# Fixed weight slots, in-place raw operands and earlier bank sums in the second MLP product of a hybrid decoder trunk

## The chip, the cores and the metric

The kernel runs on one core of one Trainium2 chip. The metric is device time in microseconds (us) of that core, from the first instruction to the last. Five engines work beside each other: PE multiplies matrices, DVE (vector), ACT (scalar) and POOL work on tiles, and SP does nothing here but issue DMAs. Each engine takes its instructions in the order in which the program lists them; an instruction that waits on another engine or on a DMA holds up all that stand behind it on its own engine.

## The reference

One layer of a decoder trunk: token mixing (pooling, gated DeltaNet and convolution heads between an input and an output projection), then an MLP, then a final normalisation. The change touches the last two:

```python
hf = _rmsnorm(x, g_norm2) * (1 + scale2) + shift2
a = jax.nn.relu(hf @ w_ff1)                 # (2048, 1024) @ (1024, 4096)
x = x + gate2 * ((a * a) @ w_ff2)           # (2048, 4096) @ (4096, 1024)
y = _rmsnorm(x, g_final)                    # x * rsqrt(mean(x*x)) * g_final
```

Everything is fp32. A second input of 8 single rows (the samples) goes through the same weights.

## The kernel before, in words

The two MLP products are done in the Winograd form of Strassen's method: a 2x2 block product takes 7 products (P1, P6, P5, P7, P2, P3, P4) of sums of blocks in place of 8. Each fp32 operand is split in two halves, a rounded high part (an ACT copy) and the rest as low part (a DVE subtraction), and each product is 3 matmuls (high x high, high x low, low x high).

The second product (`a*a` times `w_ff2`) runs in 8 passes (`nb`) over the hidden dimension. A pass takes two row groups of weights (`q` = 0 and 1) and goes over 8 tiles of the output (`gi`, `j`). So there are 64 blocks (function `block`) of 7 products x 2 q x 3 = 42 matmuls of 128x128 by 128x512. The 7 products of a block share four PSUM banks `ps_x`, `ps_y`, `ps_v`, `ps_z`, in the order x, y, v, z, x, v, z; when a bank is done, DVE adds it to a running sum in SBUF (`acc`, `accu`), and only then may the next product use that bank.

What a block reads:

- The weights of the pass, 2 x 7 tiles `wo` of 128x2x512 (B11, B21, B22 and sums T1 to T4). `w2_load` fetches the raw rows, `w2_samples` uses them for the samples (small matmuls into `ps_s`) and scales them by the gate on POOL (L1686), and `w2_ops` makes the sums (POOL, in place) and splits them (ACT cast L1401, DVE subtraction L1398). Each `wo` takes the next slot of a ring of 20 (`RING2`, through `entry`): with 14 tiles a pass, a tile of the next pass reuses the slot of one that the current pass may still be reading.
- The activations, tiles `ai` for each (tile, q), double buffered, two DMAs each (products 0 to 3, products 4 to 6). Where `early` holds (q = 0 nearly always) they come from DRAM already split. For the other half, `a_load` fetches the raw sums into a buffer `af` of its own (double buffered), and ACT and DVE split them into `ai` (L1759, L1398).

In the last pass the first two products' sum `accu` is added to `c22` on DVE and to `c12` and `c21` on POOL. Then the tiles that are finished go in groups through `final`: squares with row sums on ACT (L1798), the inverse root on DVE (a chain of some 13 small instructions), a multiplication by `gf` (the gains `g_final`) on POOL for one half, scaling on ACT (L1816) and DVE (L1818), and an output DMA. `gf`, and `gs`, `accs`, `xr` of the samples, live in the same memory slots as some of the weights (pool `r2`, tag "o", 9 slots before).

A scheduler sets the order of every engine's list: it runs the program through its own model of time and takes, of what is ready there, what has the highest priority (`tc.high_priority`); a tile whose slot is not yet free in that model is not ready.

Of the kernel before, what the change touches and what calls it, by code (L numbers as in the profile page):

```python
# [9 lines left out]
F32 = mybir.dt.float32  # L10
F32R = mybir.dt.float32r
# [6 lines left out]
P = 128  # L18
D = 1024
# [25 lines left out]
XB = 11  # L45
AO = 4
WE = 4
TB = 10
R2 = 9
XS = 1000  # L50
ORDER = ["gp01kq23"] * 4
RSQRT_MAGIC = 1597463007.0
# [9 lines left out]
def hybrid_trunk(  # L62
# [1311 lines left out]
    with ExitStack() as ph2:  # L1374
# [66 lines left out]
        a32 = f1.tile([P, 2, 2, 32], F32, name="a32")  # L1441
        Q.memset(a32, 0.0)
        chunks = f1.tile([P, 256], F32, name="chunks")
        xsT = f1.tile([P, KT, 32], F32, name="xsT")
        Q.memset(xsT, 0.0)


# [99 lines left out]
        def entry(slots):  # L1547
            pool, tag = slots[ring[0] % len(slots)]
            ring[0] += 1
            return pool.tile([P, 2, 512], F32R, tag=tag, name="wo")  # L1550

        RING1 = [(wp, "whi"), (wp, "wlo"), (we, "e"), (we, "e"), (wp, "whi"), (wp, "wlo")] + [(we, "e")] * (WE - 2)

# [105 lines left out]
        KB = 2  # L1659
        NB = NP // KB  # L1660
        halves = (slice(0, 512), slice(512, 1024))
        RING2 = [(wp, "whi")] + [(ao, "a")] * AO + [(xpool, "x"), (wp, "wlo"), (wp, "whi"), (wp, "wlo")]

        def w2_load(p, pool=None):
            raws = []
# [19 lines left out]
                for raw in raws:  # L1685
                    Q.tensor_tensor(out=raw, in0=raw, in1=g2, op=ALU.mult)  # L1686

        def w2_ops(raws):

            with tc.high_priority(offset=HP):  # L1690
                return right_ops(*(raw[:, s] for raw in raws for s in halves), lambda o: entry(RING2))

        with tc.high_priority(offset=800):
            xs_ops = [x_ops_first(j) for j in range(4)]
# [6 lines left out]
        for gi in range(2):  # L1701
            for p in range(NP):
                w_now = w
                if gi == 0 or p < NP - 1:
                    raws = w1_load((p + 1) % NP)
                    if srow:
                        sample_rows(*srow)
                        srow = None
                    if gi or p == NP - 1:
                        srow = sample_unit((p + 1) % NP, raws)  # L1710
                    w = w1_ops(raws)
                if p == 0 and gi:
                    with tc.high_priority(offset=XS):
                        xs_ops = x_second()
                    c = unit(w_now, xs_ops)
                elif p == 0:
                    c = unit_by_k(w_now, lambda j: xs_ops[j])
                else:
                    if gi and p == NP - 1:
                        g2 = xpool.tile([P, D], F32, tag="x", name="g2")  # L1720
                        for k in range(KT):
                            nc.sync.dma_start(out=g2[:, k * P:(k + 1) * P], in_=g2_scr[k, 8:9, :].to_broadcast([P, P]))
                        ring[0] = 0
                        first2 = [w2_load(0), w2_load(1, xpool)]
                        for q in range(KB):
                            w2_samples(q, first2[q])
                        w2 = [w2_ops(first2[0])]
                    c = unit(w_now, xs_ops)
                a_ops(gi, p, c)
                if gi and p == NP - 1:  # L1730
                    sample_rows(*srow)
                if gi == 0 and p in (2, 6, 10):
                    later = (x_later(0), x_later(1), x_sums())[p // 4]
                for _ in later:
                    break
                if gi == 0 and p == 14:
                    xt = load_rows(x1_scr[T:T + NS, :], NS)
                    A.activation(out=xt[:NS], in_=xt[:NS], func=AF.Copy, scale=rs2[:NS, 16:17])
                    full = sample_act(xt, 3, lambda: psa.tile([P, KT, NS], F32, tag="b", name="ps_hs"))
                    V.tensor_copy(out=xsT[:, :, 0:NS], in_=full)  # L1740

        ff1_pools.close()
        ai = ph2.enter_context(tc.tile_pool(name="ai", bufs=2))
        r2 = ph2.enter_context(tc.tile_pool(name="r2", bufs=R2))
        sm = ph2.enter_context(tc.tile_pool(name="sm3", bufs=2))
        ac = ph2.enter_context(tc.tile_pool(name="ac", bufs=1))
        RING2 += [(r2, "o")] * R2 + [(xpool, "x")] * 2

        def a_load(gi, j, p):

            es = [ai.tile([P, n_, 2, P], F32R, tag=f"i{p % 2}{h}", name=f"ai{h}", bufs=2) for h, n_ in enumerate((4, 3))]
            if early(gi, p):
                for e, o in zip(es, (slice(0, 4), slice(4, 7))):
                    nc.sync.dma_start(out=e.bitcast(F32).rearrange("p o a t -> p o (a t)"), in_=a_scr[gi][p][:, j, o])
            else:
                raw = ai.tile([P, 7, P], F32, tag="f", name="af", bufs=2)
                nc.sync.dma_start(out=raw, in_=a_scr[gi][p][:, j])
                for e, o in zip(es, (slice(0, 4), slice(4, 7))):
                    A.copy(out=e[:, :, 0, :], in_=raw[:, o])  # L1759
                    sub(V, e[:, :, 1, :], raw[:, o], e[:, :, 0, :])  # L1760
            return es

        acc = {}
# [10 lines left out]
        def block(nb, gi, j, w, a):  # L1774

            b = {n: bank("ps_" + n) for n in "xyvz"}
            rows, u = acc[gi, j]
            c11, c12, c21, c22 = (r[:, s] for r in rows for s in halves)
            into = {0: u, 1: u, 2: c22, 3: c22, 4: c11, 5: c12, 6: c21}
            for n, ((l, r), name, first, last) in enumerate(PRODUCTS):  # L1780
                ps = b[name]
                for q in range(KB):
                    for i, (x, y) in enumerate(PAIRS):
                        nc.tensor.matmul(out=ps, lhsT=a[q][n // 4][:, n % 4, x, :], rhs=w[q][r][:, y, :],  # L1784
                                         start=first and q == 0 and i == 0, stop=last and q == KB - 1 and i == 2,
                                         skip_group_check=True)
                if n == 0 and nb == 0:
                    A.copy(out=u, in_=ps)
                else:
                    add(V, into[n], ps, into[n])  # L1790
                if n == 1 and nb == NB - 1:
                    add(V, c22, c22, u)
                    add(Q, c12, c12, u)
                    add(Q, c21, c21, u)

        def square_sum(x, out):
            junk = ai.tile([P, 512], F32, tag="junk", name="junk", bufs=1).bitcast(BF16)[:, 0:x.shape[-1]]
# [22 lines left out]
                    nc.sync.dma_start(out=dst[:, s], in_=x[:m, s])  # L1820

        def samples_out():
            gs, accs, xr = (r2.tile([P, D], F32, tag="o", name=n) for n in ("gs", "accs", "xr"))
            nc.sync.dma_start(out=gs[0:NS].rearrange("j (k p) -> j k p", k=KT),
                              in_=g2_scr[:, 0:NS, :].rearrange("k j p -> j k p"))
            for j in range(4):
                nc.sync.dma_start(out=accs[0:NS, 256 * j:256 * j + 256], in_=chunks[32 * j:32 * j + NS])
            load_rows(x1_scr[T:T + NS, :], NS, xr)
            Q.tensor_tensor(out=accs[:NS], in0=accs[:NS], in1=gs[:NS], op=ALU.mult)
            add(V, accs[:NS], accs[:NS], xr[:NS])  # L1830
            final([(accs, NS, y_sample.rearrange("b t d -> (b t) d"))])

        tiles = [(gi, j) for gi in range(2) for j in range(4)]
        w = [w2[0], w2_ops(first2[1])]
        done = []
        steps = [(nb, gi, j) for nb in range(NB) for gi, j in tiles]
        a = [a_load(0, 0, q) for q in range(KB)]
# [1 line left out]
        for i, (nb, gi, j) in enumerate(steps):  # L1839
            a_now, w_now = a, w  # L1840
            if i + 1 < len(steps):
                nb2, gi2, j2 = steps[i + 1]
                a = [a_load(gi2, j2, KB * nb2 + q) for q in range(KB)]
                if nb2 == 0:
                    acc_load(gi2, j2)
            if nb + 1 < NB:
                at = i % len(tiles)
                if at == 0:
                    w_next = []
                if at in (0, 3):  # L1850
                    raws = w2_load(KB * (nb + 1) + at // 3)
                elif at in (2, 5):
                    w2_samples(KB * (nb + 1) + at // 3, raws)
                    w_next.append(w2_ops(raws))
                elif at == len(tiles) - 1:
                    w = w_next
            block(nb, gi, j, w_now, a_now)
            if nb == NB - 1:
                if i == len(steps) - len(tiles):
                    gf = r2.tile([P, D], F32, tag="o", name="gf")  # L1860
                    nc.sync.dma_start(out=gf, in_=g_final.unsqueeze(0).to_broadcast([P, D]))
                if i == len(steps) - len(tiles) + 1:
                    samples_out()
                done += [(acc[gi, j][0][th], P, y_prompt[0, t * P:(t + 1) * P, :])
                         for th, t in enumerate((8 * gi + j, 8 * gi + 4 + j))]
                if j % 2 or gi and j == 2:
                    final(done)
                    done = []
# [27 lines left out]
```

## Time and profile before

| | us |
|---|---|
| three timed runs, median | 2512.17 (2507.35 to 2512.51) |
| profiled execution | 2506.09 |
| its span | 2504.4 |
| first matmul of the second product starts at | 1795.71 |
| last group of 6 matmuls of the second product | 2489.03 to 2491.79 |
| last work of DVE and ACT ends at | about 2500.0 |

Busy shares over the span are PE 95%, DVE 76%, ACT 44%, POOL 28%. The second product takes the last 28% of the span. Times below are from the start of the span. Up to the second product nothing but line and buffer numbers differs between the two kernels' lists, so it is the stretch from 1795 on that has to be read.

### The profile page before, as it was taken

The numbers are of one execution on the slowest core, as the hardware profiler recorded it, in microseconds if no ns is written. First come the engines' busy times: TensorE is split into PE (matmuls) and PEld (weight loads), VectorE is DVE, ScalarE is ACT, GpSimd is POOL, SyncE is SP. The second block draws the span as 40 slices with busy tenths as digits, with TensorE's granted clock in tenths as the row PEclk, the third lists the DMA queues.
The fourth block names the chain that finished last, engine by engine and source line by source line (L and its number), as shares of the span: only waits on it lengthen the run. The fifth ranks groups of instructions, "written<-read, shape, count | busy, mean of one in ns | idle before, by whom it ended". The sixth has DMA issues, their size and how long they took to land. (4 is left out here: it accounts for less than half of the span.)

```text
span 2504.4 us, 36348 instructions
## 1 busy us (share of the span) xinstructions
PE 2369.7 (95%) x12797; PEld 1887.6 (75%) x12797; DVE 1902.9 (76%) x3378; ACT 1092.1 (44%) x2411; POOL 697.9 (28%) x469
## 2 busy tenths in 40 slices
PE   7988999999999999989999999999899999999996
PEld 4566788788999788667877767777677777778775
DVE  3986987887887576677788786766777777777788
ACT  3266247237336443456565665555432112211224
POOL 2101101021111234543236422223513222322254
PEclk9999999999999999999999999999999999999998
DMA  9986534544543567844779785656655455545455
GB/s 326 352 278 226 171 122 167 175 144 160 210 137 131 147 198 228 269 156 147 249 229 324 252 266 156 206 160 197 213 222 168 156 165 158 157 151 159 157 172 178
DMA packets 406150, 490.72 MB, mean 196 GB/s; under 512 B 39082, under 2 KB 306027, under 8 KB 405944
## 3 DMA queue, kind: packets, MB, share of 16 engines
q1 hardware_dynamic: 331120, 386.55, 47.5%
q10 hardware_dynamic: 73088, 96.48, 11.8%
q0 software_dynamic: 1760, 5.38, 0.7%
q8 instruction: 101, 1.65, 0.3%
q14 instruction: 81, 0.66, 0.1%
HBM read 335.63 MB, written 153.07 MB: 195 GB/s over the span
## 5 line engine op out<-in xcount | busy, mean ns | idle before, releaser
L179 PE MATMUL ps_ip<-hhi,whi 128*128 128x512 f32 (+1 forms) x1112 | 411.7, 371 | 11.5 <-ACT whi L150 9.0
L179 PE MATMUL ps_ip<-hhi,wlo 128*128 128x512 f32 (+1 forms) x1112 | 409.8, 369 | 4.9 <-DVE wlo L131 4.9
L179 PE MATMUL ps_ip<-hlo,whi 128*128 128x512 f32 (+1 forms) x1112 | 409.4, 369 | 4.4 <-DVE hlo L131 3.4
L179 PEld LDWEIGHTS ps_ip<-hhi,whi 128*128 128x128 f32 x1112 | 211.6, 190 | 53.4 <-ACT whi L150 11.1
L179 PEld LDWEIGHTS ps_ip<-hhi,wlo 128*128 128x128 f32 x1112 | 211.7, 190 | 45.5 <-DVE wlo L131 10.2
L179 PEld LDWEIGHTS ps_ip<-hlo,whi 128*128 128x128 f32 x1112 | 211.7, 190 | 38.7 <-DVE hlo L131 5.2
L1784 PE MATMUL ps_v<-wo,ai 128*128 128x512 f32 x768 | 203.4, 396 | 19.0 <-DVE acc L1395 10.1
L1401 ACT CAST wo<-raw 128x512 fp32r<-128x512 f32 x208 | 125.6, 618 | 197.4 <-POOL raw L1398 62.6
L1759 ACT CAST ai<-af 128x384 fp32r<-128x384 f32 (+1 forms) x128 | 72.2, 568 | 316.5 <-PE ps_z L1784 268.6
L1784 PE MATMUL ps_x<-wo,ai 128*128 128x512 f32 x768 | 201.1, 401 | 5.8 <-DVE accu L1395 2.6
L1398 DVE TENSOR_TENSOR wo<-raw,wo 128x512 fp32r<-128x512 f32 x208 | 190.7, 930 | 16.3 <-ACT wo L1401 15.8
L1784 PE MATMUL ps_z<-wo,ai 128*128 128x512 f32 x768 | 200.9, 395 | 0.6 <-DVE acc L1395 0.4
L1686 POOL TENSOR_TENSOR raw<-raw,g 128x1024 f32<-128x1024 f32 x32 | 79.5, 2504 | 413.4 <-PE ps_s L1678 195.7
L1570 PE MATMUL ps_v<-xo,wo 128*128 128x512 f32 x744 | 186.5, 398 | 6.0 <-DVE t L1395 4.0
L551 DVE SCALAR_TENSOR_TENSOR dc<-glu,dww,dc 128x512 f32<-128x512 f32 x240 | 190.1, 820 | 1.7
L1398 DVE TENSOR_TENSOR wo<-s,wo 128x512 fp32r<-128x512 f32 x128 | 122.4, 961 | 88.8 <-ACT wo L1401 87.6
L1784 PEld LDWEIGHTS ps_v<-wo,ai 128*128 128x128 f32 x768 | 144.7, 190 | 55.1 <-DVE acc L1395 13.1
L1570 PE MATMUL ps_x<-xo,wo 128*128 128x512 f32 x744 | 185.2, 396 | 0.7 <-ACT s L1611 0.7
L1570 PE MATMUL ps_z<-xo,wo 128*128 128x512 f32 x744 | 183.2, 394 | 2.5 <-DVE t L1395 2.5
L1784 PEld LDWEIGHTS ps_x<-wo,ai 128*128 128x128 f32 x768 | 145.7, 192 | 46.8 <-DVE accu L1395 4.4
L1784 PEld LDWEIGHTS ps_z<-wo,ai 128*128 128x128 f32 x768 | 145.5, 190 | 34.7 <-DVE acc L1395 2.4
L1570 PEld LDWEIGHTS ps_v<-xo,wo 128*128 128x128 f32 x744 | 138.5, 189 | 41.6 <-DVE t L1395 6.0
(503 smaller groups left out, 4709.6 us busy)
## 6 DMA issues: line engine op xcount, KB each, us to landing
a_scr<-ae SPq DMA_DIRECT2D x112, 512.0 KB
raw<-in_w_ff SPq DMA_DIRECT2D x94, 512.0 KB
whi<-w_scr ACTq DMA_DIRECT2D x66, 512.0 KB
wlo<-w_scr ACTq DMA_DIRECT2D x66, 512.0 KB
ai<-a_scr SPq DMA_DIRECT2D x64, 512.0 KB
af<-a_scr SPq DMA_DIRECT2D x64, 448.0 KB
mraw<-in_w_ada SPq DMA_DIRECT2D x48, 512.0 KB
ai<-a_scr SPq DMA_DIRECT2D x64, 384.0 KB
```

What stands on the lines that cost most here:

```text
L179: nc.tensor.matmul(out=ps, lhsT=a[:, k, :], rhs=b, start=(i == 0), stop=(i == 3 * KT - 1))
L551: nc.vector.scalar_tensor_tensor(out=d, in0=gt[:, j:j + GT], scalar=dww[:, t, j:j + 1], in1=d, op0=ALU.mult, op1=ALU.add)
L1398: eng.tensor_tensor(out=out, in0=in0, in1=in1, op=ALU.subtract)
L1401: A.copy(out=entry[:, 0, :], in_=full)
L1570: nc.tensor.matmul(out=ps, lhsT=w[:, a, c], rhs=x[:, b, :], start=start and i == 0, stop=stop and i == 2, skip_group_check=True)
L1686: Q.tensor_tensor(out=raw, in0=raw, in1=g2, op=ALU.mult)
L1759: A.copy(out=e[:, :, 0, :], in_=raw[:, o])
L1784: nc.tensor.matmul(out=ps, lhsT=a[q][n // 4][:, n % 4, x, :], rhs=w[q][r][:, y, :], start=first and q == 0 and i == 0, stop=last and q == ...
```

## The change

It does six things, all in the second product:

1. The ring goes. A pass has fixed slots by its parity: `DOUBLED[0]` for even passes, `DOUBLED[1]` for odd ones, 9 slots each, for the 7 tiles of q = 0 and for B11 and T2 of q = 1. The other five tiles of q = 1 have one slot each (tags s0, s1, ...) for all passes. "o" has 7 slots instead of 9.
2. The raw rows of the next pass are loaded at blocks 1 and 3 of a pass instead of 0 and 3 and used at 2 and 5 as before; in the first pass they are loaded at 1 and 4 and used at 3 and 6.
3. `a_load` has no `af`: the raw sums go by two DMAs straight into the low half of `ai`, ACT casts from there to the high half, and DVE subtracts in place.
4. In the last pass the bank adds on DVE get a priority of 400.
5. There, the add of `accu` to `c22` comes after product 4 instead of after product 1.
6. The tile `xsT` moves to another pool; `gf`, `gs`, `accs`, `xr` stay in tag "o", of which an odd pass, as the last one is, uses all 7.

```diff
-R2 = 9
+R2 = 7
+LP = 400
-        RING2 = [(wp, "whi")] + [(ao, "a")] * AO + [(xpool, "x"), (wp, "wlo"), (wp, "whi"), (wp, "wlo")]
+        DOUBLED = [[(wp, "whi")] + [(ao, "a")] * AO + [(xpool, "x"), (wp, "wlo"), (wp, "whi"), (wp, "wlo")]]
...
-        def w2_ops(raws):
+        def w2_ops(n, raws):
+            slots = DOUBLED[n // KB % 2]
+            b11, b12, b21, b22 = (raw[:, s] for raw in raws for s in halves)
             with tc.high_priority(offset=HP):
-                return right_ops(*(raw[:, s] for raw in raws for s in halves), lambda o: entry(RING2))
+                if n % KB == 0:
+                    ring[0] = 0
+                    return right_ops(b11, b12, b21, b22, lambda o: entry(slots))
...
+                t = ai.tile([P, 512], F32, tag="junk", name="t2", bufs=1)
+                put(B11, b11, slots[7])
+                sub(Q, b11, b12, b11)
+                sub(Q, b12, b22, b12)
+                sub(Q, t, b22, b11)
+                put(T2, t, slots[8])
+                sub(Q, t, b21, t)
+                for o, full in ((T1, b11), (T3, b12), (B21, b21), (B22, b22), (T4, t)):
+                    put(o, full, (r2, f"s{o}"))
+                return out
...
-        r2 = ph2.enter_context(tc.tile_pool(name="r2", bufs=R2))
+        r2 = ph2.enter_context(tc.tile_pool(name="r2", bufs=1))
-        RING2 += [(r2, "o")] * R2 + [(xpool, "x")] * 2
+        DOUBLED.append([(r2, "o")] * 5 + [(xpool, "x")] * 2 + [(r2, "o")] * 2)
...
-                raw = ai.tile([P, 7, P], F32, tag="f", name="af", bufs=2)
-                nc.sync.dma_start(out=raw, in_=a_scr[gi][p][:, j])
-                for e, o in zip(es, (slice(0, 4), slice(4, 7))):
-                    A.copy(out=e[:, :, 0, :], in_=raw[:, o])
-                    sub(V, e[:, :, 1, :], raw[:, o], e[:, :, 0, :])
+                    nc.sync.dma_start(out=e32[:, :, 1, :], in_=a_scr[gi][p][:, j, o])
+                    A.copy(out=e[:, :, 0, :], in_=e32[:, :, 1, :])
+                    sub(V, e[:, :, 1, :], e32[:, :, 1, :], e[:, :, 0, :])
...
-                    add(V, into[n], ps, into[n])
-                if n == 1 and nb == NB - 1:
-                    add(V, c22, c22, u)
+                    with tc.high_priority(offset=LP if nb == NB - 1 else 0):
+                        add(V, into[n], ps, into[n])
+                if nb == NB - 1 and n == 1:
                     add(Q, c12, c12, u)
                     add(Q, c21, c21, u)
+                if nb == NB - 1 and n == 4:
+                    add(V, c22, c22, u)
...
-            gs, accs, xr = (r2.tile([P, D], F32, tag="o", name=n) for n in ("gs", "accs", "xr"))
+            gs, accs, xr = (r2.tile([P, D], F32, tag="o", name=n, bufs=R2) for n in ("gs", "accs", "xr"))
...
-                if at in (0, 3):
-                    raws = w2_load(KB * (nb + 1) + at // 3)
-                elif at in (2, 5):
+                loads, uses = ((1, 4), (3, 6)) if nb == 0 else ((1, 3), (2, 5))
+                if at in loads:
+                    raws = w2_load(KB * (nb + 1) + loads.index(at))
+                elif at in uses:
...
-                    gf = r2.tile([P, D], F32, tag="o", name="gf")
+                    gf = r2.tile([P, D], F32, tag="o", name="gf", bufs=R2)
```

SP's list in the last pass of the kernel before (`a_scr_14` and `a_scr_15` are the activations of the last pass, `out` the results) has the loads of `gf`, `gs`, `accs` and `xr` among the loads of the first tiles, and the first results between later loads:

```order
L1754 DMA ai_22108<-a_scr_14_11322 128x1024
L1861 DMA gf<-in_g_final 128x1024
L1824 DMA gs<-g_scr 8x8x128
L1827 DMA accs<-chunks 8x256 x3
L1754 DMA ai_22112<-a_scr_15_11323 128x1024
L1827 DMA accs<-chunks 8x256
L193 DMA xr<-x_scr 8x1024
L1754 DMA ai_22261<-a_scr_14_11322 128x1024
...
L1754 DMA ai_22445<-a_scr_14_11338 128x1024
L1820 DMA out<-acc_17762 128x512 x2
L1820 DMA out<-acc_17764 128x512 x2
```

In the changed kernel SP has them behind the last load of activations, after everything else of the pass:

```order
L1779 DMA ai_22525<-a_scr_15_11339 128x4x128
L1777 DMA ai_22522<-a_scr_14_11338 128x768
L1779 DMA ai_22526<-a_scr_15_11339 128x3x128
L1777 DMA ai_22641<-a_scr_14_11338 128x1024
L1779 DMA ai_22645<-a_scr_15_11339 128x4x128
L1777 DMA ai_22642<-a_scr_14_11338 128x768
L1779 DMA ai_22646<-a_scr_15_11339 128x3x128
L1885 DMA gf<-in_g_final 128x1024
L1847 DMA gs<-g_scr 8x8x128
```

What moved: `gf` from ahead of the second tile's activations to behind the last tile's. In the last pass the seven "o" slots hold weights of that pass, and each of the four tiles gets one only when a product of the last block has read it.

ACT's list in the last pass of the kernel before has squares (`junk,fv`) and scalings (`nr_y`) between the casts of the activations:

```order
L1759 CAST ai_22449<-af 128x4x128
L1816 ACTIVATE acc_17762<-acc_17762,nr_y 128x512
L1816 ACTIVATE acc_17764<-acc_17764,nr_y 128x512
L1816 ACTIVATE acc_17779<-acc_17779,nr_y 128x512
L1816 ACTIVATE acc_17781<-acc_17781,nr_y 128x512
L1798 ACTIVATE junk,fv<-acc_17924 128x512 x2
L1759 CAST ai_22450<-af 128x3x128
L1798 ACTIVATE junk,fv<-acc_17926 128x512 x2
```

In the changed kernel the last cast comes first, and then all 34 squares and all 17 scalings in one row (its first lines):

```order
L1780 CAST ai_22525<-ai_22525 128x4x128
L1780 CAST ai_22526<-ai_22526 128x3x128
L1780 CAST ai_22645<-ai_22645 128x4x128
L1780 CAST ai_22646<-ai_22646 128x3x128
L1821 ACTIVATE junk,fv<-accs 8x512 x2
L1821 ACTIVATE junk,fv<-acc_17763 128x512 x2
L1821 ACTIVATE junk,fv<-acc_17765 128x512 x2
L1821 ACTIVATE junk,fv<-acc_17780 128x512 x2
L1821 ACTIVATE junk,fv<-acc_17782 128x512
```

What moved: every square and scaling of the final normalisation, from between the blocks of the last pass to behind its last load.

PE's list at the start of the second product, before (`ai_17754` and `ai_17771` are q = 1 of the first two tiles, `ps_s` the samples):

```order
L1784 MATMUL ps_x<-wo,ai_17754 128x512
L1784 MATMUL ps_x<-wo,ai_17771 128x512 x3
L1678 MATMUL ps_s_17929<-raw_17784,a_11341 32x256
L1678 MATMUL ps_s_17929<-raw_17786,a_11341 32x256
...
L1784 MATMUL ps_y<-wo,ai_17754 128x512
L1784 MATMUL ps_y<-wo,ai_17771 128x512
L1784 MATMUL ps_y<-wo,ai_17754 128x512 x2
```

and in the changed kernel (there the two are `ai_17755` and `ai_17772`):

```order
L1805 MATMUL ps_x<-wo,ai_17755 128x512
L1805 MATMUL ps_y<-wo,ai_17755 128x512 x2
L1805 MATMUL ps_x<-wo,ai_17772 128x512 x2
L1805 MATMUL ps_y<-wo,ai_17772 128x512 x2
L1805 MATMUL ps_x<-wo,ai_17772 128x512
L1805 MATMUL ps_y<-wo,ai_17772 128x512
L1679 MATMUL ps_s_18004<-raw_17855,a_11341 32x256
L1679 MATMUL ps_s_18004<-raw_17857,a_11341 32x256
...
L1805 MATMUL ps_v<-wo,ai_17755 128x512
L1805 MATMUL ps_z<-wo,ai_17755 128x512
```

What moved: the six matmuls of `ps_y` for q = 1 (they read the weight tile T2) now stand ahead of the samples' matmuls.

## Rows read from the trace of the kernel before

**Rows 1.** Windows: stretch, its length, busy us (count) by engine, granted clock, DMA share.
```profile
1795.00:1825.00 30.00, 19.48 (x69) 12.71 (x68) 21.05 (x30) 11.99 (x22) 15.85 (x9) 0.77 0.98 348
2066.00:2150.00 84.00, 81.21 (x370) 63.79 (x369) 62.31 (x89) 19.10 (x34) 24.43 (x15) 1.00 0.52 162
2396.00:2492.00 96.00, 80.75 (x324) 62.17 (x322) 90.16 (x152) 37.76 (x91) 53.19 (x37) 0.95 0.49 162
```

**Rows 2.** Waits of PE, 1795 to 2505: total us, times, longest.
```profile
PE ps_v L1784 <- DVE acc L1395: 10.1, 3, 5.8
PE ps_v L1784 <- DVE wo L1398: 8.8, 4, 2.8
PE ps_y L1784 <- ACT wo L1401: 4.4, 4, 2.5
PE ps_s L1678 <- DMA raw<-in_w_ff: 3.2, 1, 3.2
PE ps_x L1784 <- DVE accu L1395: 2.6, 3, 2.0
PE ps_y L1784 <- DVE wo L1398: 2.3, 2, 1.7
```

**Rows 3.** Timeline of PE and ACT, start of the second product: start, us, work.
```profile
1811.22 1.09 PE L1678 MATMUL ps_s<-raw,a 128*32 128x256 f32 x14 [3.21 <-DMA raw<-in_w_ff]
1814.12 2.18 ACT L1401 CAST wo<-raw 128x512 fp32r<-128x512 f32 x4 [8.64 <-DMA af<-a_scr]
1814.79 1.22 PE L1784 MATMUL ps_y<-wo,ai 128*128 128x512 f32 x2 [2.48 <-ACT wo L1401]
```

**Rows 4.** Timeline of DVE and PE at a change of passes.
```profile
1979.55 5.13 DVE L1398 TENSOR_TENSOR wo<-raw,wo 128x512 fp32r<-128x512 f32 x3
1984.73 0.73 PE L1784 MATMUL ps_v<-wo,ai 128*128 128x512 f32 x2 [2.76 <-DVE wo L1398]
...
1985.53 2.89 PE L1784 MATMUL ps_x<-wo,ai 128*128 128x512 f32 x12
1988.26 0.62 PE L1784 MATMUL ps_z<-wo,ai 128*128 128x512 f32 x2
```

**Rows 5.** Groups of DVE: a middle pass (2066 to 2150), then the last (2400 to 2505).
```profile
L1398 DVE TENSOR_TENSOR wo<-raw,wo 128x512 fp32r<-128x512 f32 x16 | 17.3, 1106 | 2.4 <-ACT wo L1401 2.3
...
L1395 DVE TENSOR_TENSOR acc<-acc,accu 128x512 f32<-128x512 f32 x8 | 12.3, 1553 | 0.1
L1395 DVE TENSOR_TENSOR acc<-ps_v,acc 128x512 f32<-128x512 f32 x16 | 10.8, 683 | 1.6 <-PE ps_v L1784 1.5
```

**Rows 6.** Chain that ended last: issue of an activation load, us to its landing.
```profile
2305.02 3.59 DMA ai<-a_scr
2417.24 3.79 DMA ai<-a_scr
```

**Rows 7.** Waits of SP's queue, 1795 to 2400.
```profile
SPq L1754 <- PE ps_z L1784: 260.3, 87, 6.7
```

**Rows 8.** Timeline of ACT and groups of POOL, last pass: squares, scalings, `gf` multiplications.
```profile
2426.15 0.63 ACT L1798 ACTIVATE junk<-acc 128x512 bf16<-128x512 f32 x1
2426.90 0.63 ACT L1798 ACTIVATE junk<-acc 128x512 bf16<-128x512 f32 x1
2440.85 2.56 ACT L1816 ACTIVATE acc<-acc,nr_y 128x512 f32<-128x512 f32 x4 [4.74 <-DVE nr_y L123]
...
L1809 POOL TENSOR_TENSOR acc<-acc,gf 128x512 f32<-128x512 f32 x16 | 21.3, 1334 | 25.4 <-ACT junk L1798 25.2 <-DVE nr_a L121 0.2
```

**Rows 9.** Timeline of the end.
```profile
2489.03 2.76 PE L1784 MATMUL ps_z<-wo,ai 128*128 128x512 f32 x6
2493.47 7.73 SPq L1820 DMA_DIRECT2D out<-acc  x8
2495.27 0.16 DVE L1395 TENSOR_TENSOR sq<-fv 128x2 f32<-128x2 f32 x1 [1.17 <-ACT junk L1798]
2498.66 1.33 ACT L1816 ACTIVATE acc<-acc,nr_y 128x512 f32<-128x512 f32 x2 [3.42 <-DVE nr_y L123]
```

More of the change, by code (lines that the diff above doesn't have):

```diff
@@ L1443, in hybrid_trunk @@
         chunks = f1.tile([P, 256], F32, name="chunks")
-        xsT = f1.tile([P, KT, 32], F32, name="xsT")
+        xsT = sm.tile([P, KT, 32], F32, name="xsT", bufs=1)
         Q.memset(xsT, 0.0)
@@ L1549, in entry @@
             ring[0] += 1
-            return pool.tile([P, 2, 512], F32R, tag=tag, name="wo")
+            return pool.tile([P, 2, 512], F32R, tag=tag, name="wo", **({"bufs": R2} if tag == "o" else {}))
         RING1 = [(wp, "whi"), (wp, "wlo"), (we, "e"), (we, "e"), (wp, "whi"), (wp, "wlo")] + [(we, "e")] * (WE - 2)
@@ L1686, in w2_samples, with put @@
                     Q.tensor_tensor(out=raw, in0=raw, in1=g2, op=ALU.mult)
-        def w2_ops(raws):
+        def w2_ops(n, raws):
+            slots = DOUBLED[n // KB % 2]
+            b11, b12, b21, b22 = (raw[:, s] for raw in raws for s in halves)
             with tc.high_priority(offset=HP):
-                return right_ops(*(raw[:, s] for raw in raws for s in halves), lambda o: entry(RING2))
+                if n % KB == 0:
+                    ring[0] = 0
+                    return right_ops(b11, b12, b21, b22, lambda o: entry(slots))
+                out = {}
+                def put(o, full, pool_tag):
+                    pool, tag = pool_tag
+                    out[o] = pool.tile([P, 2, 512], F32R, tag=tag, name="wo", **({"bufs": R2} if tag == "o" else {}))
+                    split(out[o], full)
+                t = ai.tile([P, 512], F32, tag="junk", name="t2", bufs=1)
[8 more added lines that the diff above has]
+                return out
         with tc.high_priority(offset=800):
@@ L1726, in hybrid_trunk @@
                             w2_samples(q, first2[q])
-                        w2 = [w2_ops(first2[0])]
+                        w2 = [w2_ops(0, first2[0])]
                     c = unit(w_now, xs_ops)
@@ L1743, in hybrid_trunk @@
         ai = ph2.enter_context(tc.tile_pool(name="ai", bufs=2))
-        r2 = ph2.enter_context(tc.tile_pool(name="r2", bufs=R2))
+        r2 = ph2.enter_context(tc.tile_pool(name="r2", bufs=1))
         sm = ph2.enter_context(tc.tile_pool(name="sm3", bufs=2))
         ac = ph2.enter_context(tc.tile_pool(name="ac", bufs=1))
-        RING2 += [(r2, "o")] * R2 + [(xpool, "x")] * 2
+        DOUBLED.append([(r2, "o")] * 5 + [(xpool, "x")] * 2 + [(r2, "o")] * 2)
         def a_load(gi, j, p):
             es = [ai.tile([P, n_, 2, P], F32R, tag=f"i{p % 2}{h}", name=f"ai{h}", bufs=2) for h, n_ in enumerate((4, 3))]
-            if early(gi, p):
-                for e, o in zip(es, (slice(0, 4), slice(4, 7))):
-                    nc.sync.dma_start(out=e.bitcast(F32).rearrange("p o a t -> p o (a t)"), in_=a_scr[gi][p][:, j, o])
-            else:
-                raw = ai.tile([P, 7, P], F32, tag="f", name="af", bufs=2)
-                nc.sync.dma_start(out=raw, in_=a_scr[gi][p][:, j])
-                for e, o in zip(es, (slice(0, 4), slice(4, 7))):
-                    A.copy(out=e[:, :, 0, :], in_=raw[:, o])
-                    sub(V, e[:, :, 1, :], raw[:, o], e[:, :, 0, :])
+            for e, o in zip(es, (slice(0, 4), slice(4, 7))):
+                e32 = e.bitcast(F32)
+                if early(gi, p):
+                    nc.sync.dma_start(out=e32.rearrange("p o a t -> p o (a t)"), in_=a_scr[gi][p][:, j, o])
+                else:
+                    nc.sync.dma_start(out=e32[:, :, 1, :], in_=a_scr[gi][p][:, j, o])
+                    A.copy(out=e[:, :, 0, :], in_=e32[:, :, 1, :])
+                    sub(V, e[:, :, 1, :], e32[:, :, 1, :], e[:, :, 0, :])
             return es
@@ L1833, in hybrid_trunk @@
         tiles = [(gi, j) for gi in range(2) for j in range(4)]
-        w = [w2[0], w2_ops(first2[1])]
+        w = [w2[0], w2_ops(1, first2[1])]
         done = []
@@ L1849, in hybrid_trunk @@
                     w_next = []
-                if at in (0, 3):
-                    raws = w2_load(KB * (nb + 1) + at // 3)
-                elif at in (2, 5):
-                    w2_samples(KB * (nb + 1) + at // 3, raws)
-                    w_next.append(w2_ops(raws))
+                loads, uses = ((1, 4), (3, 6)) if nb == 0 else ((1, 3), (2, 5))
+                if at in loads:
+                    raws = w2_load(KB * (nb + 1) + loads.index(at))
+                elif at in uses:
+                    w2_samples(KB * (nb + 1) + uses.index(at), raws)
+                    w_next.append(w2_ops(KB * (nb + 1) + uses.index(at), raws))
                 elif at == len(tiles) - 1:
```

## The prediction

> **What bounds the kernel now.** I read the windows first, to see which engine is full in which stretch. In a middle pass of the second product PE is busy 81 of 84 us at the full granted clock, DVE 62; from 2396 to 2492, the last pass, DVE is busy 90 of 96 us while PE's clock falls to 0.95 of full [rows 1]. So PE sets the time in the middle, and at two kinds of places something else does. The waits of PE say which: bank sums on DVE (`acc`, 10.1 us in three waits), weight splits on DVE and ACT (8.8, 4.4, 2.3), the `accu` add (2.6), one load of raw weights (3.2) [rows 2]. The timelines then place them: the start, the change of passes, the last pass, the end.
>
> A matmul takes 0.2275 us at full clock: 12 start between 1985.53 and 1988.26 [rows 4]. A block of 42 is 9.55 us, a product (6 matmuls) 1.37.
>
> **The last pass.** In it DVE does the finals of finished tiles between the bank sums, and the adds `acc<-acc,accu` take 1.55 us on average where a sum out of PSUM takes 0.68 [rows 5]. The windows count 324 matmuls from 2396 to the last start near 2491.2: 95.2 us, of which 324 x 0.2275 = 73.7 is work [rows 1]. 21.5 us are lost; about 2.6 of them belong to the change of passes at its beginning, as the one of the same kind in rows 4. So 19 us are lost to DVE and to the clock, which is low after the stalls. In the changed list all finals stand behind the last block, so that DVE has, in a block, 7 sums (4.8 us), one `c22` add and two splits of activations, 7.4 us together, against 9.55. I leave 3 us for what comes late there: gain 16, bounds 10 and 19.
>
> **The change of passes.** Splits for the next pass wait until the current one has read the slot they go to: three DVE splits take 5.13 us and PE waits 2.76 for them [rows 4]. By rows 2 such waits sum to 8.8 + (4.4 - 2.5) + (2.3 - 1.7) + 2.6 = 13.9 us, the 2.5 and 1.7 being those of the start; with the restart of PE and the low clock behind the longest I put 16. With two sets, 9 of 14 tiles never wait for the current pass. The other five are read last in the q = 1 half of the last block and are needed one block later, 39 matmuls (8.9 us) after, against 0.62 + 0.69 us of splitting. What could be late next is DVE, which then has these five on top of the sums. I leave 2: gain 14, bounds 4 and 16.
>
> **The start.** Here ACT waits 8.64 us, until 1814.12, for memory that the first product still uses, and PE waits 3.21 for raw weights and 2.48 for the splits [rows 3]. In the changed list T2 of q = 1 no longer has one of those slots, so 30 second-product matmuls stand ahead of the samples' in place of 24; the load of raw weights and the slots of T1 and T3 are as late as before. Gain 6 x 0.45 (the clock is low there, 0.77 [rows 1]) = 2.7; bounds -2 and 9.
>
> **Raw activations in place.** Without `af` the load can only start when PE has read the old tile. PE itself need not wait: release to next use is 51 matmuls, 11.6 us. The loads that wait so today (260.3 us in 87 waits, hidden) [rows 7] take 3.6 to 3.8 us from issue to landing [rows 6]; the new ones are half their size, and in the list each goes right behind a larger one on the same queue. The cost is in DVE's list: the split of the second tile stands there ahead of a bank sum that is due 13 matmuls (3.0 us) after the release. With 3.6 for the landing, 0.1 for the issue, 0.6 for the cast and 0.6 for the split the sum starts at 4.9, 1.9 us late. A bank has two or three products (2.7 or 4.1 us) until its next use, less 0.68 for the sum: slack 2.0 or 3.4. So a block without weight splits just carries it. In the blocks with them (seven splits at 1.1 us [rows 5] beside 4.8 us of sums) DVE has no spare time, and some of it reaches PE. Bounds: 0 if the loads land in under 3 us, and 64 x 0.3 = 19 us if every one is a little over the slack. I take 5, nearer the lower, since the new loads are smaller than those of rows 6. The second DMA of each pair, 64 more issues on SP at about 0.3 us, lies in SP's idle time.
>
> The Trainium skill, "DMA: Bandwidth & Descriptors", Anatomy of one DMA, gives 2.0 us plus bytes at 436 GB/s: an estimate of 2.6 and 2.5 us for the new loads, by which this term would be 0 and the sum 5 us lower. For the loads of rows 6 the same rule gives 2.9 to 3.2 where the trace has 3.6 to 3.8, so it is low here by some 0.6; its figure was for another path of issue.
>
> **The end.** This is what speaks against the change. Today the last matmuls end at 2491.8, and only two tiles remain: chain of small DVE instructions from 2495.27, scalings until 2500.0, outputs, span end 2504.4: 12.6 us [rows 9]. In the changed list `gf`, `gs`, `accs` and `xr` get their "o" slots only when products of the last block have read the weights in them, and ACT's first square waits for `xr`. `xr`'s slot is free 30 matmuls (6.8 us) before PE's end; 3.6 for the load and about 2 for the samples' multiplication and add put the first square at -1 us. Then ACT has in one row 34 squares at 0.75 us (start to start) and 17 scalings at 2.56/4 = 0.64 [rows 8]: 25.5 + 10.9 = 36.4. Near the end it waits for the last chain, 3.4 us [rows 9], of which two scalings of the group before cover 1.3. So ACT ends at -1 + 36.4 + 2.1 = 37.5, and with the same 4.4 to the span's end the tail is 41.9, 29.3 longer. POOL's 16 multiplications by `gf` (21.3 us) [rows 8] now run beside the chains, which makes some of them late: I add 2, so 31. Bounds 25 (the chains hidden, first square 3 us earlier) and 38 (each of five chains 1.5 us longer). DVE's wait for `xr` stands ahead of the last block's sums too: 1 us on PE.
>
> The Trainium skill, "GPSIMD Engine Reference", Key points, says that POOL shares its SBUF interfaces with DVE and contends with instructions that read two SBUF inputs. The trace agrees (1.55 against 0.68 us [rows 5], the latter reading PSUM). By that rule the 16 scalings on DVE that read `gf` would slow as well; at 1.55 each they are 25 us beside ACT's 36, and the sum does not change.
>
> **The sum.** PE: -16 - 14 - 2.7 + 5 + 1 = -27 us. End: +31. Net +4 us on the profiled execution (2506.09, span 2504.4), 2510. That execution is 6 us under the median of the runs; carried over to the median, 2512 + 4 = 2516.
>
> **Rivals.**
> *The gain outweighs the end.* If the start's waits go as a whole (9), the raw loads land in under 3 us (0 in place of 5) and passes change without a wait (16): -19 - 16 - 9 + 1 = -43, with the end at +30: -13, 2499. For it: PE's waits are all on things that the lists now have earlier. Against it: at the start both the raw load and the memory of the first product are as late as before.
> *The in-place loads hold up DVE.* If the landing is 3.6 or more every time, most of the 64 splits block DVE past the banks' slack: 19 in place of 5, net +18, 2530. It decides from a landing of about 3.7 us on. For it: rows 6. Against it: half the bytes.
> *The slots only move the wait.* DVE is full in the block before each change of passes, and the five single-slot tiles are split there; if PE waits as long as before, the gain of 14 falls to 3: +15, 2527.
>
> **Chances.** The forecast, between -3 and +10, has 0.42; the first rival 0.30, the second 0.18, the third 0.10. What a measurement of this kernel can tell from no change is about 0.2%, 5 us. The forecast's case splits into 0.04 faster, 0.19 within, 0.19 slower; the first rival is faster but for 0.02, the other two slower but for 0.02: faster 0.32, same 0.23, slower 0.45. For 8 in 10 the range takes in the first rival with 3 us to spare and the second with 5: 2496 to 2535. The forecast's own range is 2509 to 2522.
>
> **What would show it.** Last pass: no PE wait on `acc` over 1 us and DVE's load well under PE's. Changes of passes: no waits on `wo` over 1 us. The end: PE ends near 2465, ACT's squares lie in one row behind it, and some 42 us pass to the end of the span. DVE's waits on ACT's `ai` casts show the price of the in-place loads. I am wrong on the main point if a good part of the finals runs before PE's end, or if the second product on PE isn't shorter by at least 15 us.

## The result and the profile after

The changed kernel takes 2496.14 us (median of 6 runs, 2489.5 to 2497.09) against 2511.6 for the kernel before in the same session: a ratio of 0.9943 [0.9929, 0.9956]. I had forecast 0.2% slower; it is 0.6% faster. The profiled executions (2506.09 and 2489.5, each below the median of its kernel) differ by 16.6 us, the medians by 15.5. Of the two big terms both came out larger than I had them: PE gained 49 us in the second product and not 27, the end lost 36 and not 31.

The matmul records are complete (2688 of the second product in each trace), so the two traces can be laid side by side by count, each stretch from the start of its first matmul to that of the next stretch's:

| us | before | after | difference | forecast |
|---|---|---|---|---|
| start of the span to the first matmul of the second product | 1795.7 | 1791.65 | -4.1 | 0 |
| matmuls 1 to 336 | 97.9 | 97.2 | -0.7 | -2.7 |
| 337 to 2352 (six passes) | 499.4 | 472.4 | -27.0 | -14 + 5 |
| 2353 to the start of the last | 98.1 | 76.9 | -21.2 | -16 + 1 |
| from there to the span's end | 13.2 | 49.6 | +36.4 | +31 |
| span | 2504.4 | 2487.8 | -16.6 | +4 |

I don't count the first line as an effect: up to there the instructions of all kernels are the same, and in the ten runs of the experiments below the second product starts anywhere from 1794.3 to 1801.3. The changed kernel's 1791.65 lies below all of them, so its profile flatters it by a few us; the other lines don't depend on this.

The windows of the changed kernel, of two middle stretches, the last pass and the end, with the columns of [rows 1]:

```profile
1900.00:1985.00 85.00, 85.00 (x408) 68.44 (x406) 64.84 (x96) 18.19 (x32) 23.20 (x14) 1.00 0.56 168
1985.00:2066.00 81.00, 81.00 (x382) 65.72 (x379) 61.20 (x90) 17.94 (x31) 24.82 (x15) 1.00 0.55 166
...
2361.00:2439.00 78.00, 76.86 (x338) 63.00 (x336) 51.27 (x75) 8.37 (x17) 25.22 (x18) 1.00 0.45 137
2439.00:2488.00 49.00, 0.00 (x0) 0.00 (x0) 37.44 (x91) 32.59 (x79) 20.56 (x17) 0.52 0.46 172
```

PE is busy without a gap in the middle, at the full clock. In the last pass DVE, at 90 of 96 us before [rows 1], has 51 of 78. The last 49 us have no matmul at all, and DVE and ACT do the finals there. The waits of PE, to be read against [rows 2]:

```profile
PE ps_s L1679 <- DMA raw<-in_w_ff: 2.9, 1, 2.9
PE ps_v L1805 <- DVE wo L1399: 1.9, 2, 1.3
PE ps_x L1805 <- DMA ai<-a_scr: 1.7, 1, 1.7
PE ps_z L1805 <- DVE wo L1399: 1.5, 1, 1.5
...
PE ps_z L1805 <- DVE acc L1396: 0.7, 1, 0.7
```

The first four of these lie in the first pass, the last one in the last block. Six middle passes take 78.73 us each.

**The middle: part of the gain was no wait.** Those six passes have 42.2 us above 336 x 0.2268 us of work (the pace of a matmul where nothing holds PE up) before and 15.2 after. Of the 27 us, the matmuls at which PE waited come to 11.9 (10.5 of it idle). The low clock behind two of the waits is 3.2: 16 matmuls start 0.43 us apart, and from 2237 to 2239 the granted clock is 0.50, the lower of its two levels. Another 3.2 are single matmuls that start up to 0.15 us late, near half of it right behind the samples' matmuls. The other 8.7 are the samples' matmuls `ps_s` themselves. Before, in each set of 8 (but for the first, which came in three pieces) one stood alone, 12 to 128 matmuls ahead of the other 7 (the timeline shows two records for each):

```profile
1942.86 0.62 PE L1678 MATMUL ps_s<-raw,a 128*32 128x256 f32 x2
...
1972.65 1.08 PE L1678 MATMUL ps_s<-raw,a 128*32 128x256 f32 x14
```

After, the eight stand together:

```profile
1983.99 1.09 PE L1679 MATMUL ps_s<-raw,a 128*32 128x256 f32 x16
```

A visit of one costs 0.64 us above the pace, more than half of the 1.11 of a whole set: two split sets cost a pass 3.49 us and two whole ones 2.22. No view of waits shows this, since PE is never idle for a releaser there.

**The last pass: the late splits had been in it.** DVE's groups in the last pass of the kernel before held, beside the sums of [rows 5], seven splits of that pass's own weights, which had waited for slots (before, 2396 to 2492):

```profile
L1398 DVE TENSOR_TENSOR wo<-raw,wo 128x512 fp32r<-128x512 f32 x7 | 8.7, 1270 | 0.1
L1818 DVE SCALAR_TENSOR_TENSOR acc<-acc,nr_y,gf 128x512 f32<-128x512 f32 x12 | 8.2, 746 | 0.0
```

In the changed kernel (2361 to 2439) two of them are left, no scaling, and the `c22` adds take half their time:

```profile
L1396 DVE TENSOR_TENSOR acc<-acc,accu 128x512 f32<-128x512 f32 x8 | 6.1, 769 | 0.2
...
L1399 DVE TENSOR_TENSOR wo<-raw,wo 128x512 fp32r<-128x512 f32 x1 | 0.7, 694 | 0.0
L1399 DVE TENSOR_TENSOR wo<-t,wo 128x512 fp32r<-128x512 f32 x1 | 0.7, 682 | 0.0
```

**The loads in place** land as late as I had put them, and PE does not feel it. Of the casts from 1900 to 2360, 78 wait for their load; from its issue to the start of the cast it is 3.03 to 6.86 us, 3.7 in the median. In the timelines of SP, ACT and DVE of a middle pass the load issued at 2049.00 is what the cast at 2052.24 waits for, 3.24 us; the load before it took 3.82 (2042.43 to 2046.25). DVE then waits 1.30 us for the cast with a bank sum behind it:

```profile
2049.00 0.37 SPq L1779 DMA_DIRECT2D ai<-a_scr  x1
...
2052.24 0.51 ACT L1780 CAST ai<-ai 128x384 fp32r<-128x384 f32 x1 [2.56 <-DMA ai<-a_scr]
2052.79 0.56 DVE L1399 TENSOR_TENSOR ai<-ai 128x384 fp32r<-128x384 f32 x1 [1.30 <-ACT ai L1780]
2053.26 0.68 DVE L1396 TENSOR_TENSOR acc<-ps_z,acc 128x512 f32<-128x512 f32 x1
```

From 1900 to 2360 DVE waits like this 68 times, 83.6 us in all, and PE has no wait in that stretch: the banks' slack takes it. The estimate of 2.5 to 2.6 us from the rule of the Trainium skill ("DMA: Bandwidth & Descriptors", Anatomy of one DMA) is too low for these loads; the measurement decides.

**The end.** ACT's groups from 2436 to 2488, with the idle time before them at the right:

```profile
L1821 ACT ACTIVATE junk<-acc 128x512 bf16<-128x512 f32 x32 | 20.1, 628 | 0.9
L1839 ACT ACTIVATE acc<-acc,nr_y 128x512 f32<-128x512 f32 x16 | 10.3, 711 | 9.7 <-DVE nr_y L124 5.7 <-DVE sq L188 2.1 <-DVE sq L1396 1.9
...
L1821 ACT ACTIVATE junk<-accs 8x512 bf16<-8x512 f32 x2 | 1.3, 629 | 11.2 <-DVE accs L1396 11.2
L1839 ACT ACTIVATE accs<-accs,nr_y 8x512 f32<-8x512 f32 x1 | 0.7, 721 | 1.3 <-DVE nr_y L124 1.3
```

From the first square to the end of the last scaling it is 47.1 us (2436.32 to 2483.39), of which 11.0 are waits: the squares and scalings are the 36 us that were forecast. What I had too small is the 9.7 + 1.3 us for which scalings wait for DVE's chains; I had 2.1 for the last chain and 2 for the others.

### The profile page after: what moved, and what is told of

Its sections match the earlier page's. It is cut to its first block, busy times and chain, and to the rows that moved or that the text cites. A ratio compares the mean times of both kernels' runs of the same rounds, so it can differ in the third digit from the quotient of the medians.

```text
span 2487.8 us, 36542 instructions
## 1 busy us (share of the span) xinstructions
PE 2340.6 (94%) x12797; PEld 1879.6 (76%) x12797; DVE 1892.3 (76%) x3378; ACT 1093.8 (44%) x2411; POOL 692.1 (28%) x469
## 5 line engine op out<-in xcount | busy, mean ns | idle before, releaser
L1780 ACT CAST ai<-ai 128x512 fp32r<-128x512 f32 (+1 forms) x128 | 72.3, 567 | 350.0 <-DMA ai<-a_scr 334.4
L1805 PE MATMUL ps_v<-wo,ai 128*128 128x512 f32 x768 | 197.6, 391 | 2.4 <-DVE wo L1399 1.9
L1805 PE MATMUL ps_x<-wo,ai 128*128 128x512 f32 x768 | 195.3, 395 | 1.7 <-DMA ai<-a_scr 1.7
L1402 ACT CAST wo<-raw 128x512 fp32r<-128x512 f32 x192 | 116.5, 619 | 152.3 <-POOL raw L1399 41.1
L1399 DVE TENSOR_TENSOR ai<-ai 128x512 fp32r<-128x512 f32 (+1 forms) x128 | 100.8, 789 | 104.9 <-ACT ai L1780 104.6
```

The costliest lines, as they stand in the source:

```text
L1399: eng.tensor_tensor(out=out, in0=in0, in1=in1, op=ALU.subtract)
L1402: A.copy(out=entry[:, 0, :], in_=full)
L1780: A.copy(out=e[:, :, 0, :], in_=e32[:, :, 1, :])
```

## The experiments

Theory after the result: the gain comes from three more slots (23 instead of 20), for which the memory of `af` pays, and the loss at the end only from `gf`, `gs`, `accs` and `xr` sharing "o" slots with the last pass. Rivals: the fixed order by product and parity, the later loads, or the priority of the bank sums make the gain; the end is the price of the shorter last pass.

All in one table (stretches as above; ratio to the kernel before in the same session, with its 95% interval):

| kernel | ratio | 337 to 2352 | 2353 to last | end |
|---|---|---|---|---|
| before | 1 | 499.4 | 98.1 | 13.2 |
| changed | 0.9943 [0.9929, 0.9956] | 472.4 | 76.9 | 49.6 |
| e_fin | 0.9840 [0.9814, 0.9866] | 474.2 | 84.3 | 13.5 |
| e_fin_nolp | 0.9840 [0.9814, 0.9865] | 472.4 | 86.3 | 15.4 |
| e_ring | 0.9997 [0.9982, 1.0013] | 475.9 | 75.9 | 53.0 |
| b_lp | 0.9989 [0.9973, 1.0005] | 501.0 | 95.6 | 13.6 |
| b_inplace | 1.0026 [1.0008, 1.0043] | 509.3 | 95.0 | 15.1 |
| b_slots12 | 0.9973 [0.9957, 0.9989] | 476.6 | 75.9 | 50.2 |
| e_gf_o | 0.9886 [0.9860, 0.9912] | 472.4 | 84.8 | 28.2 |
| e_fin_load0 | 0.9821 [0.9788, 0.9855] | 472.4 | 83.5 | 13.4 |
| e_fin_load0_b | 0.9838 [0.9818, 0.9858] | 472.4 | 83.9 | 13.8 |
| e_group | 0.9829 [0.9808, 0.9851] | 472.4 | 79.3 | 17.4 |

**e_fin**, the changed kernel with the four tiles elsewhere:

```diff
-gf = r2.tile([P, D], F32, tag="o", name="gf", bufs=R2)
+gf = ao.tile([P, D], F32, tag="a", name="gf", bufs=AO)
-gs, accs, xr = (r2.tile([P, D], F32, tag="o", name=n, bufs=R2) ...
+gs, accs, xr = (ao.tile([P, D], F32, tag="a", name=n, bufs=AO) ...
```

> The changed kernel, with gf, gs, accs and xr in the four 'a' slots, which belong to the even passes and are free in the last (odd) one. Theory: the 49 us from PE's end to the span's end come only from the finals waiting for the 'o' slots. Then the finals go back between the blocks of the last pass, the end falls to 13 to 20 us, PE's last pass stays within 4 us of the changed kernel's 77, and the time is 28 to 34 us under the changed kernel's 2496: 2462 to 2468. Rival: the last pass lost its stalls only because the finals had left it; then they come back (15 to 21 us on PE) and the time is 2478 to 2486.

It took 2469.96 us, 2 us above the range of the theory, and 1.6% under the kernel before. The end is back at 13.5, as forecast; PE's last stretch is 7.4 us longer than in the changed kernel, where the theory allowed 4. The windows of its last pass and end:

```profile
2370.00:2455.00 85.00, 80.05 (x337) 64.29 (x336) 73.64 (x140) 35.98 (x87) 45.00 (x33) 0.96 0.59 194
2455.00:2468.00 13.00, 0.00 (x0) 0.00 (x0) 7.58 (x25) 4.11 (x8) 2.22 (x2) 0.63 0.43 161
```

DVE carries the finals and is busy 74 of 85 us, not 90 of 96. So most of what the last pass gained (14 of 21 us) has nothing to do with the finals being gone from it.

**e_fin_nolp**, e_fin without the priority and with `c22` after product 1:

```diff
-with tc.high_priority(offset=LP if nb == NB - 1 else 0):
-    add(V, into[n], ps, into[n])
+add(V, into[n], ps, into[n])
-if nb == NB - 1 and n == 4:
+if nb == NB - 1 and n == 1:
     add(V, c22, c22, u)
```

> As e_fin, but without the priority of the bank sums in the last pass and with the c22 add after product 1 as in the kernel before. Theory: with the finals between the blocks these two are what keeps PE from waiting: the last pass takes 10 to 20 us longer than in e_fin, as in the kernel before. Rival: the stalls of the last pass came from weights and slots, not from the order of the sums: within 3 us of e_fin.

2470.4 us, the same as e_fin; the last stretch is 2 us longer in the profile. The rival holds.

**b_lp**, the other way round: the kernel before with only these two edits.

> The kernel before with only the priority of the bank sums in the last pass and the later c22 add. Theory: the last pass falls from 98 us by 10 to 16, the end stays near 13 us: 2496 to 2502. Rival: the finals on DVE are as much work as before and the pass gains under 4 us: 2508 to 2512.

0.9989 [0.9973, 1.0005]: no change that can be told. Here, too, the rival holds, and the two experiments together say that parts 4 and 5 of the change are worth nothing measurable.

**e_ring**, the changed kernel with one ring over all slots:

```diff
-R2 = 7
+R2 = 12
...
-slots = DOUBLED[n // KB % 2]
+slots = sum(DOUBLED, [])
...
-if n % KB == 0:
-    ring[0] = 0
+if True:
+    ring[0] *= n > 0
...
-DOUBLED.append([(r2, "o")] * 5 + [(xpool, "x")] * 2 + [(r2, "o")] * 2)
+DOUBLED.append([(r2, "o")] * R2 + [(xpool, "x")] * 2)
```

> The changed kernel with one rotating ring again, over all its slots (23 instead of the 20 of the kernel before, 'o' has 12); all else as changed. Theory A: what counts at the changes of passes is how many slots are spare (9 of 23); middle passes take 78.7 to 80 us, as in the changed kernel. Theory B: the fixed sets by product and parity count: middle passes take 81 to 84 us as before, 15 to 30 us over the second product. The end stays over 40 us, as xr still waits for the last block.

Theory A: the middle passes take 78.7 or 79.9 us. The three of 79.9 have one set of samples' matmuls in two pieces, which costs 1.06 us more than in one. The fixed sets give 3.5 us in the middle and 5 in the first pass, and the ring loses them and 3 more at the end: as fast as before in all. So the slots make PE's gain, but the rival is right for a part of it: without the fixed order, worth some 11 us here, the change would not have been faster.

**b_inplace**, the kernel before with the raw activations loaded in place.

> The kernel before with only the raw activations loaded in place (no af, two DMAs that wait for PE). Theory: DVE's wait for the cast costs PE nothing, since the bank sums have slack: middle passes stay at 82 to 85 us and the time within 5 us of before. Rival (my prediction's term): where the weight splits fall, the wait reaches PE: middle passes 1 to 3 us longer each, 5 to 19 us in all.

0.26% slower, the rival: the six passes take 10 us more. The waits of PE that it has more than [rows 2]:

```profile
PE ps_v L1783 <- DVE wo L1398: 11.7, 4, 4.3
PE ps_x L1783 <- DVE accu L1395: 7.9, 4, 3.2
PE ps_x L1783 <- DMA ai<-a_scr: 6.1, 3, 2.5
PE ps_z L1783 <- DVE acc L1395: 4.0, 3, 2.7
```

The third row lies in the first pass and the fourth in the last. In the six passes PE waits 17.7 us where it was 10.5, nearly all of it some 25 matmuls behind a change of passes. There the weight splits crowd: in the middle passes six or seven of the 14 of a pass run on DVE in its first 15 us, beside the casts that DVE waits for. In the changed kernel two of the 14 do, the others are spread out, and PE does not wait.

**b_slots12**, b_inplace with more slots (and `xsT` moved to make room):

```diff
-R2 = 9
+R2 = 12
```

> b_inplace with 12 'o' slots instead of 9 (a ring of 23), the loads, the priority and the c22 add as before. Theory: three more slots give the whole gain at the changes of passes: middle passes fall to 78.7 to 80 us; the finals now wait for 'o' slots and the end grows from 13 to about 50 us, so the time is within 8 us of before although PE ends 40 us earlier. Rival: loads and uses at later blocks or fixed sets are needed too: middle passes over 81 us.

As the theory had it: 476.6 us in the middle, PE's end 42 us earlier than in the kernel before, the end 50.2 us, and so 0.27% off the time. This is the whole change but for some 8 us (0.9973 and 0.9943), not far from what the fixed sets give by e_ring: in place +10, three slots -33 in the middle and -19 in the last pass, the end +35.

**e_gf_o**, the changed kernel with only `gf` left in "o".

> The changed kernel with gs, accs and xr in free 'a' slots, gf still in 'o'. Theory: xr holds up the squares and gf the multiplications and scalings; with xr early the squares (25 us of ACT) go between the blocks, and with gf late 17 scalings (11 us on ACT) and POOL's 16 multiplications (21 us, 1.33 each) stay behind PE: end 25 to 32 us, time 17 to 24 us under the changed kernel: 2472 to 2479. Rival: gf alone makes the end: 45 us or more, time as the changed kernel's.

The end is 28.2 us, as forecast; the time, 2481.7, misses the forecast by 3, since the last pass is 84.8 us where 77 had been taken for granted. The late `xr` (with `gs` and `accs`) costs some 21 us of the end and `gf` the other 15.

**e_fin_load0**, e_fin with the loads and uses of the kernel before:

```diff
-loads, uses = ((1, 4), (3, 6)) if nb == 0 else ((1, 3), (2, 5))
+loads, uses = ((0, 3), (2, 5))
```

> e_fin with the raw weights loaded and used at the blocks of the kernel before (0 and 3, 2 and 5) in all passes. Theory: the blocks of loading do not matter once the slots are there: middle passes 78.7 us, time within 4 us of e_fin (2470). Rival: the later loads keep the samples' matmuls in one piece: middle passes 80 us or more, 5 to 10 us over e_fin.

> e_fin_load0 again, beside e_group. As then: about 0.982 of before. Were the earlier blocks of loading worth something by themselves, it would be 0.2% or more under e_fin's 0.984 again; were they worth nothing, 0.982 to 0.986.

0.9821 (4.6 us under e_fin, just over the 4 forecast) and, run again, 0.9838, beside 0.9840 for e_fin: no difference, and the samples' sets are whole (78.73 us a pass). So the blocks of loading are worth nothing either; they are not what keeps the sets together.

**e_group**, e_fin_load0 with larger groups of finals:

```diff
-if j % 2 or gi and j == 2:
+if (j >= 2 if gi else j % 2):
```

> e_fin_load0 with the third and fourth group of finals joined (tiles 1,0 to 1,2 together). Theory: the 3.9 us wait of PE in the last block, with the low clock behind it, comes from the four scalings (2.74 us) that stand on DVE ahead of the last block's bank sums; with the larger group they go behind the sums: PE's last 84 matmuls take 19 to 21 us instead of 25.5, the end grows by 2 to 5 us, and the time falls by 1 to 4 us. Rival: another late sum takes their place, and the end grows too: 0 to 4 us slower.

In e_fin_load0 PE's last wait and what DVE does then, from the timelines:

```profile
2439.23 2.74 DVE L1841 SCALAR_TENSOR_TENSOR acc<-acc,nr_y,gf 128x512 f32<-128x512 f32 x4
2441.89 0.68 DVE L1396 TENSOR_TENSOR acc<-ps_z,acc 128x512 f32<-128x512 f32 x1
...
2443.82 2.93 PE L1805 MATMUL ps_v<-wo,ai 128*128 128x512 f32 x6 [3.88 <-DVE acc L1396]
```

In e_group this wait is gone, though PE waits 1.79 us for another sum six matmuls later; the last 84 matmuls take 21 us instead of 25.4, and the end is 3.6 us longer: 0.9829 against 0.9838 in the same session, not to be told apart. Part of the theory is shown (the scalings were what PE waited for), the rival is right that another late sum comes behind them, and the gain is given back at the end.

The fastest kernels are e_fin, e_fin_nolp, e_fin_load0 and e_group, 1.6 to 1.8% under the kernel before and some 1% under the changed one.

## Why the prediction was wrong

- *The change of passes (gain 14, bounds 4 and 16)* is the step that failed: with the in-place term (+5) I had the six middle passes 9 us shorter, and they are 27 shorter. I priced it from the waits of PE alone, and those came out right (11.9 us of waits and 3.2 of clock in these passes). What had no row among the waits was left out: the samples' matmuls that came in two pieces (8.7) and the small delays of single matmuls (3.2). The excess over the pace, counted by pass, would have shown them; I did that count for the last pass only.
- *Raw activations in place (5, bounds 0 and 19)*: 0. The landing was right (3.7 us in the median), and so was the wait of DVE; b_inplace shows the 10 us where the splits crowd. What I missed is that the change itself takes the crowd away: I priced the part with the old distribution of the splits. My slack was too small as well: I had a landing of about 3.7 us decide for the second rival (19 us), and about half of the loads take that long or longer, none of them with a wait of PE behind it.
- *The last pass (gain 16, bounds 10 and 19)*: 21, of which some 2.6 is the wait at its beginning that I had counted with the changes of passes. The mechanism was half wrong. I put it on the finals leaving; e_fin has them back and still gains 14. The seven late weight splits, a matter of slots again, had been in it; no run takes these splits alone, so that they make the 14 is read from DVE's groups, not shown.
- *The priority and the later `c22` add* I had counted as part of that; they are worth nothing (e_fin_nolp, b_lp).
- *The start (gain 2.7)*: 0.7. Right as to its being nearly unchanged.
- *The end (+31, bounds 25 and 38)*: +36.4, with the mechanism as told, shown by e_fin (13.5 us) and e_gf_o (28.2). Too small was what the chains on DVE cost beside POOL.
- *The first rival* (PE -43, end +30, net -13) is what happened, with -49 and +36, but not for its reasons: 9 us of it were to come from the start, which gave 0.7, and 5 from loads that land in under 3 us, which none of the 78 did, though the 5 came. The changes without a wait it had right; the samples' matmuls stood in for the start. That its net came near is luck.

In sum, a net of two terms near 30 us each was forecast from terms known to some 10 us; the sign was open, as the chances (0.32 for faster) said, and both were undersized.

## What to carry to other kernels

Count what a stage takes above its work at the full pace, and make the parts of a forecast add up to it; what no wait explains (a short matmul group visited twice) was found in no other way here. A buffer that is borrowed from a rotating pool for the tail of a program is only as early as the last user of that pool: see first which slots the last stage leaves idle. When memory is traded between parts, price each part with the others in place, since an added wait that costs 10 us alone (b_inplace) may cost nothing once its neighbours are spread out.

## What the runs showed of the hardware that was not expected

While POOL works on two SBUF tiles, a small DVE instruction that starts beside it can last until POOL is done. The timeline of the end of the changed kernel has this pattern in each chain but the last:

```profile
2447.32 1.27 POOL L1832 TENSOR_TENSOR acc<-acc,gf 128x512 f32<-128x512 f32 x1 [0.24 <-ACT junk L1821]
2447.34 1.27 DVE L122 TENSOR_TENSOR nr_a<-nr_y 128x4 f32<-128x4 f32 x1
...
2448.83 1.26 POOL L1832 TENSOR_TENSOR acc<-acc,gf 128x512 f32<-128x512 f32 x1 [0.24 <-ACT junk L1821]
2448.84 1.27 DVE L124 SCALAR_TENSOR_TENSOR nr_y<-nr_a,nr_y 128x4 f32<-128x4 f32 x1
...
2450.14 0.16 DVE L122 TENSOR_TENSOR nr_a<-nr_y 128x4 f32<-128x4 f32 x1
```

The two DVE instructions of 128x4 elements end within 0.02 us of POOL's, at 1.27 us, where the next of the same kind takes 0.16. Three such in a chain of 12 (the first, of 1.14 us, lies ahead of these rows) make it 5.6 us long (2445.76 to 2451.32), and ACT waits for it; the last chain of the kernel before, with one such, took 3.3 (2495.27 to 2498.60). The Trainium skill ("GPSIMD Engine Reference", Key points) says that the two share their SBUF interfaces and that DVE instructions with two SBUF inputs contend; the two rows at 1.27 us agree, and they add that a short instruction lasted as long as POOL's. And to take a set of the samples' matmuls, which have another shape, in two visits of PE cost 0.63 us (one and seven of them, in the kernel before) to 1.06 us (the other divisions, in e_ring) more than in one.
